# Right operands of w_up without their zero columns, in a transformer layer on one core

## The chip, the core and the metric

The kernel runs on one core of a Trainium2 chip. The core has a matrix engine (TensorE, "PE" in the profile; its weight loads are listed apart as "PEld"), a vector engine (DVE), an activation engine (ACT), a general engine (POOL) and a queue engine (SP) that issues the transfers here. The engines run their own instruction streams in order and wait for each other through semaphores. The metric is the device time of one execution in microseconds (us).

## The reference

One layer of a diffusion backbone is computed for 128 context tokens and 512 latent tokens, 640 in all, 1024 features wide, in float32. After an attention and convolution mixer, the second half of the layer is a feed-forward network with a short convolution over the tokens:

```
def dwconv3(x, w):
    xp = jnp.pad(x, ((0, 0), (1, 1), (0, 0)))
    return w[0] * xp[:, :-2] + w[1] * xp[:, 1:-1] + w[2] * xp[:, 2:]

def conv_ffn(u, p):
    up = dwconv3(u @ p["w_up"], p["conv_ffn"])
    g, val = jnp.split(up, 2, axis=-1)
    return (jax.nn.silu(g) * val) @ p["w_down"]
```

`w_up` is 1024 x 5632, `w_down` 2816 x 1024. The convolution pads each sequence with a zero token at both ends, and context and latent tokens are two sequences. So the rows that are convolved need a zero column ahead of the context, one between context and latent, and one behind the latent.

## The kernel before, in words

*Precision.* Every float32 operand of a large product is split into a high part, rounded to the format that PE multiplies, and a low part, the rest. A product of two such operands is three matmuls (high x high, high x low, low x high) that add up in one PSUM bank. ACT makes the high part (L1017 for weights, L1350 for right operands), DVE the low part (L1021, L1353).

*Layout.* Features lie on the partitions, tokens along the columns. The modulated and normed tokens u, transposed, are written into two tiles `UFa` and `UFb` (features 0 to 511 and 512 to 1023) by `modulated` (L1423). Each row there has `NCOL = 644` columns: a zero, the 128 context tokens, a zero, the 512 latent tokens, two zeros. Six memsets on POOL (L1330 to L1332) write the zeros. Halves of `HALF = 322` columns give four quadrants B11, B12, B21, B22 (first index: features, second: tokens).

*Products.* The 5632 outputs are handled in 22 steps j; each takes 128 columns of the gate half g and 128 of the value half of w_up. The first two (`NPLAIN = 2`) are plain: 16 blocks in all (`plain`, L1466). Steps 2 to 21 use a Strassen scheme with seven blocks instead of eight (`strassen`, L1571): A11, A12, S2, S1, S3, S4, A22 in this order, whose right operands are the quadrants or sums of them (T1 to T4). A block (`block`, L1023) is four k tiles times three matmuls, 12 matmuls of 128 x 128 weights with 322 columns, all issued by line 1030. The same line issues the blocks of an earlier Strassen stage, the projection w_in, with 320 columns (tokens without zeros).

*Banks and sums.* Of step j, two PSUM banks out of a ring of three take the results, and the intermediate results go to the rows of a tile `C` (`crows`, L1459: four rows for g, three for the value, 644 columns each): ACT copies a result to a small tile (`copied`, L1036; tags p1, u2, p5), DVE adds it to the other bank's result and writes half a row of C (`added`, L1040), and the last product of the step, A22, is copied to its half row by ACT in the next step (`last_copy`, L1653). A12 of a step writes over the bank that this copy reads.

*Behind the products.* Three steps later ACT and DVE convolve the rows: ACT multiplies by the middle tap (`tap_mid`, L1507), DVE adds the outer taps (`taps_out`, L1511), then follow silu (L1517), gate times value (`gated`, L1521) and the split of the activations (`act_hi`, `act_lo`). These read `NACT = 642` columns of C, shifted by 0, 1 and 2. From step 4 on, PE also multiplies the activations of step j - 4 by half of w_down (`down`, L1557), 15 matmuls of 512 columns, between S1 and S3. After step 21 the remaining activations and the other half of w_down follow (L1889 on).

*Order.* The instruction order on PE, ACT and DVE is the order in which the code is written (a manual schedule, L263); the copies, sums, splits and taps of a step are therefore interleaved by hand between the calls of `product`. SP's and POOL's orders are set by the framework's scheduler, and so are the waits.

*Memory.* Tiles live in regions that are reused by tag (r0 to r3, r4 to r7b); a region is as long as its longest tile, and the regions lie one behind the other. `C` takes the region of `WR` (r3) when `crows` is called for the first time, in the plain stage.

Of the kernel before, what the change touches and what calls it, by code (L numbers as in the profile page):

```python
# [11 lines left out]
F32 = mybir.dt.float32  # L12
F32R = mybir.dt.float32r
AF = mybir.ActivationFunctionType
ALU = mybir.AluOpType
# [4 lines left out]
NCTX = 128  # L20
NTOK = 640
# [3 lines left out]
NKV = 4  # L25
DFF = 2816
NJ = DFF // 128
NCOL = 644
HALF = NCOL // 2
NACT = NCOL - 2  # L30
NRING = 4
FLAG = 3
DLAG = 4
# [28 lines left out]
def trunk_layer(ctx, tc, x_prompt, x_sample, cache_k, cache_v, c, c_ctx, w_ada, b_ada, g_pre1, g_post1, g_pre2,  # L62
# [3 lines left out]
    V, S, G, PE = nc.vector, nc.scalar, nc.gpsimd, nc.tensor  # L66
# [29 lines left out]
    def region(pool, tag, shape, dtype, name):  # L96
        return pool.tile([128] + shape, dtype, tag=tag, name=name)
# [11 lines left out]
    units += [(w_in, 0, KT, O_GA + j * 128, 128) for j in range(2)] + [(w_att_out, 0, KT, j * 128, 128) for j in range(KT)]  # L109
    rest = [(w_down, 2 * q, 2, 512, 512) for q in (NJ // 2 - 2, NJ // 2 - 1, *range(NJ // 2 - 2))]  # L110
    state = {"next": 0, "raw": [], "cut": [], "limit": 10}
# [77 lines left out]
    hd = dp.tile([NT, 128, D], F32, name="hd")  # L189
    actd = dp.tile([NJ, 128, NACT], F32, name="actd")  # L190

# [73 lines left out]
    with tc.tile_pool(name="pro", bufs=2) as pro, tc.manual_schedule(engines={mybir.EngineType.SP}):  # L265
# [182 lines left out]
        for f in range(KT):  # L448
# [33 lines left out]
            if f == KT - 3:  # L482
                V.tensor_scalar(out=gains[0], in0=gains[0], scalar1=HD ** -0.5, scalar2=None, op0=ALU.mult)
                for i in range(2):
                    for a in range(2):
                        V.tensor_tensor(out=tabs[i][:, :, 0, a * 32:a * 32 + 32], in0=rt[:, :, 0, a * 32:a * 32 + 32],
                                        in1=gains[i][:, :, a * 32:a * 32 + 32].broadcast_to((128, 4, 32)), op=ALU.mult)
                        for hf in range(2):
                            d0, s0 = a * 32 + hf * 16, a * 32 + (1 - hf) * 16
                            V.tensor_tensor(out=tabs[i][:, :, 1, d0:d0 + 16], in0=rt[:, :, 1, d0:d0 + 16],  # L490
                                            in1=gains[i][:, :, s0:s0 + 16].broadcast_to((128, 4, 16)), op=ALU.mult)
            if f == KT - 2:
                cut_upto(9)
                p = ps1()
# [14 lines left out]
    with tc.tile_pool(name="att", bufs=2) as at:  # L509
# [310 lines left out]
        p = ps2()[:, 0:512]  # L820
# [41 lines left out]
        for g in range(NKV):  # L862
            if g and g + 1 < NKV:
                q_begin(g + 1)
            for i in range(0 if g else 1, 9):
# [37 lines left out]
                if blk is not None:  # L903
                    c0, c1 = 256 * blk, min(256 * blk + 256, NTOK)
# [89 lines left out]
    rb = ctx.enter_context(tc.tile_pool(name="rb", bufs=1))  # L994
# [15 lines left out]
    cut, raws, pair, TT = {}, {}, {}, {}  # L1010
# [22 lines left out]
    def temp(tag):  # L1033
        return sm_.tile([128, HALF], F32, tag=tag, name=nm(tag), bufs=1)

# [4 lines left out]
    def added(dst, j, tag, b):  # L1040
        V.tensor_tensor(out=dst, in0=pair[j][b], in1=pair.pop((j, tag)), op=ALU.add)
# [220 lines left out]
    for m, (x, i) in enumerate(PAIRS):  # L1262
# [6 lines left out]
        e, o = 2 * before[1] if m else 0, 2 * before[1] + 1 if m else 0  # L1269
# [7 lines left out]
        elif before[0] == "X":  # L1277
            c0, c1, y0, y1 = ROWS[:4]
# [7 lines left out]
        elif before[0] == "B":  # L1286
            c0, c1, y0, y1, b0, b1 = ROWS[:6]
# [36 lines left out]
    WR = region(ra, "r3", [5, D], F32, "WR")  # L1324
    TX = region(rb, "r4", [5, D], F32, "TX")

    r7 = [rb.tile([128, n], F32, tag=f"r7{x}", name=f"UF{x}") for n, x in ((4 * NCOL, "a"), (3328, "b"))]
    UFS = [x[:, 0:4 * NCOL].rearrange("p (k c) -> p k c", c=NCOL) for x in r7]
    rows3 = r7[1][:, 4 * NCOL:4 * NCOL + 256].rearrange("p (i c) -> p i c", i=2)
    for a, b in ((0, 1), (NCTX + 1, NCTX + 2), (NCOL - 2, NCOL)):  # L1330
        for x in UFS:
            G.memset(x[:, :, a:b], 0.0)  # L1332

    ZB0 = ra.tile([128, 4, 4, HALF], F32R, tag="r0", name="ZB0")
    ZB1 = ra.tile([128, 4, 4, HALF], F32R, tag="r1", name="ZB1")
# [13 lines left out]
    def right_hi(name, src, a=0, b=HALF):  # L1349
        S.activation(TT[name][0][:, :, a:b], QUAD[src][:, :, a:b], AF.Copy)  # L1350

    def right_lo(name, src, a=0, b=HALF):
        V.tensor_tensor(out=TT[name][1][:, :, a:b], in0=QUAD[src][:, :, a:b], in1=TT[name][0][:, :, a:b].bitcast(F32), op=ALU.subtract)  # L1353
# [16 lines left out]
    def ffn_taps(p):  # L1370
# [3 lines left out]

        neg = cffn.rearrange("p (d o) -> p d o", d=3)[:, :, NJ:]
        V.tensor_scalar(out=neg, in0=neg, scalar1=-1.0, scalar2=None, op0=ALU.mult)
# [39 lines left out]
    turned = {}  # L1416
# [5 lines left out]

    def modulated(t, hf):  # L1423
        row = 1 if t == 0 else 0
        c0 = 1 if t == 0 else 2 + t * 128
        for k in range(4):
            f = 4 * hf + k
            dst, src = UFS[hf][:, k, c0:c0 + 128], turned[t, hf][:, k * 128:(k + 1) * 128]
            sc, sh = mod[:, 1, row, f:f + 1], mod[:, 2, row, f:f + 1]
            if k < 3 - hf:  # L1430
                S.activation(dst, src, AF.Identity, scale=sc, bias=sh)
            else:
                V.tensor_scalar(out=dst, in0=src, scalar1=sc, scalar2=sh, op0=ALU.mult, op1=ALU.add)
# [6 lines left out]
    DBANKS = (2, 3, 4, 5, 6)  # L1440
    BANKS = {j: tuple(RING[(2 * (j - NPLAIN) + i) % 3] for i in range(2)) for j in range(NPLAIN, NJ)}
    room = {}
# [4 lines left out]
    def plain_load(j, i):  # L1447
        raws[j, i] = raw_tile()
        up_load(raws[j, i], i * NJ + j)

    def pair_load(j):
        if j < NJ:
            if "raw" not in room:
# [5 lines left out]
    def crows(j):  # L1459
        if "c" not in room:  # L1460
            room["c"] = region(ra, "r3", [7, NCOL], F32, "C")
        return room["c"][:, j % 4, :], room["c"][:, 4 + j % 3, :]

    plain_out = {}
# [5 lines left out]
        block(plain_out[j, tok, i], (j, i), step, f"B{step + 1}{tok + 1}", step == 0, step == 1)  # L1470

    def plain_copy(j, tok, i):
        dst = crows(j)[i][:, tok * HALF:(tok + 1) * HALF]
        S.activation(dst, plain_out[j, tok, i], AF.Copy, scale=(1.0, -1.0)[i])

    def sums(j):

# [93 lines left out]
    def strassen(j):  # L1571

        f, nxt = j - FLAG, j + 1 if j + 1 < NJ else None
        g = NJ - FLAG if nxt is None else None
        cg, cv = crows(j)
        pair[j] = tuple(bank(n)[:, 0:HALF] for n in BANKS[j])
        if j > NPLAIN:
            last_copy(j - 1)
        else:
            plain_copy(1, 1, 1)  # L1580
        if f >= 0:
            tap_mid(f, 0)
        lo_of((j, 1))
        product(j, "A11")

        copied(j, "p1", 0)
        if f >= 0:
            tap_mid(f, 1)
            taps_out(f, 0, (0,))
        product(j, "A12")  # L1590

        hi_of((j, 2), left(j, 2))
        added(cg[:, 0:HALF], j, "p1", 1)
        if f >= 0:
            taps_out(f, 0, (2,))
        lo_of((j, 2))
        product(j, "S2")

        copied(j, "u2", 0)
        if f >= 0:  # L1600
            silu(f)
            taps_out(f, 1)
        product(j, "S1")

        copied(j, "p5", 1)
        hi_of((j, 3), left(j, 3))
        if f >= 0:
            gated(f)
        if nxt:
            adds = sums(nxt)  # L1610
            adds[0]()
        if g:
            cut_upto(len(state["cut"]) + 1)
            tap_mid(g, 0)
            tap_mid(g, 1)
        if j >= DLAG:
            down(j - DLAG)
        product(j, "S3")

        added(cv[:, HALF:], j, "p5", 0)  # L1620
        lo_of((j, 3))
        if nxt:
            pair_load(j + 2)
            hi_of((nxt, 0), left(nxt, 0))
            lo_of((nxt, 0))
            adds[1]()
        q = max((j - DLAG + 1) // 2, 0)
        if j == NPLAIN or (j > DLAG and (j - DLAG) % 2 == 1):
            down_hi(q)
            down_lo(q)  # L1630
            down_load(q + 2 if q else 1)
            if q == 0:
                down_load(2)
        if f >= 0:
            act_hi(f)
        if g:
            act_lo(f)
            taps_out(g, 0)
            silu(g)
        product(j, "S4")  # L1640

        if nxt:
            hi_of((nxt, 1), left(nxt, 1))
        added(cg[:, HALF:], j, "u2", 1)
        if nxt:
            adds[2]()
        if g:
            taps_out(g, 1)
        elif f >= 0:
            act_lo(f)  # L1650
        product(j, "A22")

    def last_copy(j):  # L1653
        S.activation(crows(j)[1][:, 0:HALF], pair[j][0], AF.Copy)


    for row in (1, 0):
# [61 lines left out]
    for t in range(1, NT + 1):  # L1719
        if t >= 2 and t != 4:  # L1720
            normed(t - 2)
        sq_b(t - 1)
        scaled(t - 1, 1)
        for k in (0, 1):
            if t < NT:
                wo_step(t, k)
        if t == NT:
            hi_of((1, 0), raws[1, 0])
            plain(0, 0, 0, 0)
        residual(t - 1)  # L1730
        if t >= 2:
            turn2(t - 2, 0)
            modulated(t - 2, 0)
        for k in (2,):
            if t < NT:
                wo_step(t, k)
        if t == NT:
            plain(0, 0, 0, 1)
        if t >= 2:
            turn2(t - 2, 1)  # L1740
            modulated(t - 2, 1)
        sq_h(t - 1)
        if t == 3:
            right_hi("B11", "11", 0, 258)
            normed(2)
            right_lo("B11", "11", 0, 258)
        if t < NT:
            scaled(t, 0)
        if t == 3:
            right_hi("B21", "21", 0, 258)  # L1750
        if t == 4:
            right_hi("B11", "11", 258, HALF)
            right_lo("B11", "11", 258, HALF)
            right_lo("B21", "21", 0, 258)
            right_hi("B21", "21", 258, HALF)
            right_lo("B21", "21", 258, HALF)
        for k in range(3, KT):
            if t < NT:
                wo_step(t, k)
# [132 lines left out]
    w, x, y = NJ - 3, NJ - 2, NJ - 1  # L1892
# [85 lines left out]
```

## Time and profile before

| | |
|---|---|
| median of 3 runs | 1133.82 us (1132.58 to 1134.37) |
| profiled execution | 1132.64 us |
| span of its profile | 1130.9 us, granted TensorE clock 0.997 |
| w_in in Strassen form | from about 339 to 572 us |
| w_up, plain steps and steps 2, 3 | from about 699 to 744 us |
| w_up, steps 4 to 21 with half of w_down | from about 744 to 1031 us |
| rest of the activations and of w_down | from about 1031 to 1131 us |

The profile is of one execution. Its first part gives the busy time of each engine, the second the span in 40 slices, the fourth the chain of work that ended last, followed back from the end. A row of a group reads: line, engine, operation, tile written <- tiles read, shape, count | busy us, mean ns of one | idle time of the engine just before them, and who ended it. A row of the timeline or the chain reads: start in us from the span's start, length in us, then the same; a bracket behind it gives the idle time before it and its releaser. Matmul rows overlap: the listed length of one runs from its start to its modelled end, while the next one starts well before that.

### The profile page before, as it was taken

The page shows a single profiled execution, that of the slowest core. Times are in us where ns is not written, and L with a number is a line of the kernel's source. Part 1 is how long each engine was busy: PE and PEld are TensorE (multiplying, and loading weights), DVE is VectorE, ACT ScalarE, POOL GpSimd, SP SyncE. Part 2 cuts the span into 40 slices and gives each one's busy share as a digit, 9 for nine tenths or more (in the row PEclk, how much of TensorE's full clock was granted, in tenths as well). Part 3 has the DMA queues.
Part 4 walks back from the last instruction along what each step waited for, and adds up shares of the span by engine and source line. Part 5 has one row for each costly group of instructions (what it writes and reads, how often), then busy time and mean ns, then how long its engine had stood idle before and what let it go on. Part 6 is the DMA issues. An engine that isn't in the chain of part 4 may idle for free.

```text
span 1130.9 us, 19510 instructions
## 1 busy us (share of the span) xinstructions
PE 1112.9 (98%) x7885; PEld 1023.0 (90%) x7885; DVE 794.7 (70%) x1272; ACT 570.0 (50%) x979; POOL 151.5 (13%) x195
## 2 busy tenths in 40 slices
PE   7999999999999999999999999999999999999997
PEld 6787888888999999999999889999999999998786
DVE  4587666664656788889645457888887778888644
ACT  4375666665234454544532256654555455555431
POOL 2056565653000000000000012000000000000001
PEclk9999999999999999999999999999999999999999
DMA  9632433333222223323332644232333233315722
GB/s 338 204 92 79 128 95 113 104 103 113 77 71 78 76 76 96 92 75 89 100 97 77 221 149 157 67 116 88 111 105 107 90 99 106 117 61 185 244 98 93
DMA packets 177304, 129.58 MB, mean 115 GB/s; under 512 B 6274, under 2 KB 159422, under 8 KB 177214
## 3 DMA queue, kind: packets, MB, share of 16 engines
q1 hardware_dynamic: 177102, 128.30, 36.4%
q8 instruction: 62, 1.02, 0.4%
q14 instruction: 28, 0.23, 0.1%
q10 hardware_dynamic: 112, 0.04, 0.0%
HBM read 116.87 MB, written 11.45 MB: 113 GB/s over the span
## 4 chain that ended last, share of the span: by engine, by line
PE 89%; DVE 3%; ACT 1%; issue 0%; POOL 0%; DVEq 0%; POOLq 0%; ACTq 0%
PE b L1030 45%; PE b L159 9%; PE b L157 9%; PE b L158 9%; PE s L789 3%; PE s L765 3%; PE s L589 3%; PE s L157 2%; PE s L158 2%; PE s L159 2%; PE s L209 1%; DVE Y L1514 1%; DVE wlo L693 0%; PE s L560 0%; PE b L1421 0%; DVE mx L727 0%
## 5 line engine op out<-in xcount | busy, mean ns | idle before, releaser
L1030 PE MATMUL b<-ZB,whi 128*128 128x322 f32 x1024 | 228.6, 310 | 0.0
L1030 PEld LDWEIGHTS b<-ZB,whi 128*128 128x128 f32 x1024 | 173.8, 189 | 1.6
L1030 PE MATMUL b<-ZB,wlo 128*128 128x322 f32 x512 | 159.4, 311 | 0.0
L1030 PE MATMUL b<-MT,whi 128*128 128x320 f32 x608 | 134.1, 308 | 0.0
L1030 PEld LDWEIGHTS b<-MT,whi 128*128 128x128 f32 x608 | 101.6, 188 | 0.0
L1030 PEld LDWEIGHTS b<-ZB,wlo 128*128 128x128 f32 x512 | 96.2, 188 | 0.0
L1030 PE MATMUL b<-MT,wlo 128*128 128x320 f32 x304 | 93.8, 308 | 0.0
L752 POOL TENSOR_TENSOR pr<-pr,sm 128x640 f32<-128x640 f32 x64 | 80.6, 1269 | 61.2 <-DVE sm L751 61.2
L1017 ACT ACTIVATE whi<-SUM 128x1024 fp32r<-128x1024 f32 x40 | 42.2, 1055 | 79.6 <-DVE SUM L1484 77.2
L1514 DVE SCALAR_TENSOR_TENSOR Y<-C,cffn,Y 128x642 f32<-128x642 f32 x88 | 77.5, 883 | 0.9
L742 ACT ACTIVATE pr<-s,mx,rq 128x640 f32<-128x640 f32 x64 | 56.7, 886 | 38.5 <-DVE mx L729 36.4
L132 DVE TENSOR_TENSOR wlo<-raw,whi 128x1024 fp32r<-128x1024 f32 (+1 forms) x33 | 36.1, 1094 | 52.5 <-ACT whi L131 52.0
L1030 PE MATMUL b<-UH,whi 128*128 128x320 f32 x228 | 70.5, 309 | 0.0
L1030 PE MATMUL b<-UL,whi 128*128 128x320 f32 x228 | 70.4, 309 | 0.0
L1030 PE MATMUL b<-UH,wlo 128*128 128x320 f32 x228 | 70.2, 308 | 0.0
L1021 DVE TENSOR_TENSOR wlo<-raw,whi 128x1024 fp32r<-128x1024 f32 (+1 forms) x51 | 50.4, 1019 | 25.2 <-ACT whi L1017 24.3
L1017 ACT ACTIVATE whi<-WB 128x1024 fp32r<-128x1024 f32 x38 | 40.1, 1056 | 54.8 <-DVE WB L1125 54.8
L157 PE MATMUL s<-whi,UH 128*128 128x256 f32 (+1 forms) x200 | 65.9, 329 | 0.5 <-ACT UH L376 0.3
L727 DVE TENSOR_REDUCE mx<-s 128x1 f32<-128x640 f32 x64 | 52.5, 820 | 17.5 <-PE s L589 17.2
L158 PE MATMUL s<-wlo,UH 128*128 128x256 f32 (+1 forms) x200 | 61.5, 308 | 2.2 <-DVE wlo L693 2.2
L1038 ACT ACTIVATE p<-b 128x322 f32<-128x322 f32 (+1 forms) x78 | 34.3, 439 | 58.2 <-PE b L1030 58.2
L159 PE MATMUL s<-whi,UL 128*128 128x256 f32 (+1 forms) x200 | 61.8, 309 | 0.2
(319 smaller groups left out, 2922.6 us busy)
## 6 DMA issues: line engine op xcount, KB each, us to landing
raw<-in_w_in_dram SPq DMA_DIRECT2D x48, 512.0 KB, 3.7
RAW<-in_w_up_dram SPq DMA_DIRECT2D x40, 512.0 KB, 3.8
raw<-in_w_ada_dram SPq DMA_DIRECT2D x32, 512.0 KB, 3.9
raw<-in_w_down_dram SPq DMA_DIRECT2D x22, 512.0 KB, 4.0
actd<-Y SPq DMA_DIRECT2D x18, 321.0 KB, 2.6
AFB<-actd SPq DMA_DIRECT2D x18, 321.0 KB, 6.9
XT<-in_w_ada_dram SPq DMA_DIRECT2D x9, 512.0 KB, 8.7
raw<-in_w_conv_out_dram SPq DMA_DIRECT2D x9, 512.0 KB, 4.0
```

The lines of the kernel that those rows point to most:

```text
L132: V.tensor_tensor(out=lo[:, :n], in0=raw, in1=hi[:, :n].bitcast(F32), op=ALU.subtract)
L157: PE.matmul(out, ah, bh, start=start, stop=False)
L158: PE.matmul(out, ah, bl, start=False, stop=False)
L159: PE.matmul(out, al, bh, start=False, stop=stop)
L727: V.tensor_reduce(out=mx, in_=self.sc[h], axis=AX.X, op=ALU.max, negate=True)
L742: S.activation(pr, self.sc[h], AF.Exp, bias=mx, scale=rs, accum_out=sm)
L752: G.tensor_tensor(out=pr, in0=pr, in1=sm.broadcast_to((128, NTOK)), op=ALU.mult)
L1017: S.activation(to[0], raw, AF.Copy)
L1021: V.tensor_tensor(out=lo, in0=raw, in1=hi.bitcast(F32), op=ALU.subtract)
L1030: PE.matmul(out, p[:, ws], q[:, k, :], start=start and k == 0 and n == 0, stop=stop and k == 3 and n == 2, skip_group_check=True)
L1038: S.activation(t, pair[j][b], AF.Copy)
L1514: V.scalar_tensor_tensor(out=y, in0=crows(j)[i][:, d:d + NACT], scalar=cffn[:, 44 * d + o:44 * d + o + 1], in1=y, op0=ALU.mult, op1=ALU.add)
```

## The change

The right operands lose their zero columns: `UFa` and `UFb` have 640 columns, all tokens, `HALF` is 320, and each block's matmuls have 320 columns. The zeros are written only in the seven rows of `C`, once, by three memsets on POOL when C is first used. Since the first token half now holds the 128 context tokens and 192 latent tokens without the zero between them, a result for that half goes into its row in two pieces, 128 columns at column 1 and 192 at column 130 (`PARTS`); the second half is one piece of 320 at column 322. This touches the plain copies (`plain_copy`), the step's sums (`added_to` in place of `added`, for w_up only) and `last_copy`. The early splits of a part of B11 and B21 are 256 columns in place of 258. Order of the instructions, banks, transfers and counts of matmuls are as before.

```diff
+HALF = NTOK // 2
+
 NCOL = 644
-HALF = NCOL // 2
 NACT = NCOL - 2
+PARTS = (((0, 128, 1), (128, 320, 130)), ((0, 320, 322),))
...
-    r7 = [rb.tile([128, n], F32, tag=f"r7{x}", name=f"UF{x}") for n, x in ((4 * NCOL, "a"), (3328, "b"))]
-    UFS = [x[:, 0:4 * NCOL].rearrange("p (k c) -> p k c", c=NCOL) for x in r7]
...
-    for a, b in ((0, 1), (NCTX + 1, NCTX + 2), (NCOL - 2, NCOL)):
-        for x in UFS:
-            G.memset(x[:, :, a:b], 0.0)
+    r7 = [rb.tile([128, n], F32, tag=f"r7{x}", name=f"UF{x}") for n, x in ((4 * NTOK, "a"), (3328, "b"))]
+    UFS = [x[:, 0:4 * NTOK].rearrange("p (k c) -> p k c", c=NTOK) for x in r7]
...
     def crows(j):
         if "c" not in room:
             room["c"] = region(ra, "r3", [7, NCOL], F32, "C")
+            for a, b in ((0, 1), (NCTX + 1, NCTX + 2), (NCOL - 2, NCOL)):
+                G.memset(room["c"][:, :, a:b], 0.0)
...
     def plain_copy(j, tok, i):
-        dst = crows(j)[i][:, tok * HALF:(tok + 1) * HALF]
-        S.activation(dst, plain_out[j, tok, i], AF.Copy, scale=(1.0, -1.0)[i])
+        for a, b, c in PARTS[tok]:
+            S.activation(crows(j)[i][:, c:c + b - a], plain_out[j, tok, i][:, a:b], AF.Copy, scale=(1.0, -1.0)[i])
...
-        added(cg[:, 0:HALF], j, "p1", 1)
+        added_to(cg, 0, j, "p1", 1)
...
-        added(cv[:, HALF:], j, "p5", 0)
+        added_to(cv, 1, j, "p5", 0)
...
-        added(cg[:, HALF:], j, "u2", 1)
+        added_to(cg, 1, j, "u2", 1)
...
+    def added_to(row, tok, j, tag, b):
+        t = pair.pop((j, tag))
+        for a, e, c in PARTS[tok]:
+            V.tensor_tensor(out=row[:, c:c + e - a], in0=pair[j][b][:, a:e], in1=t[:, a:e], op=ALU.add)
+
     def last_copy(j):
-        S.activation(crows(j)[1][:, 0:HALF], pair[j][0], AF.Copy)
+        for a, b, c in PARTS[0]:
+            S.activation(crows(j)[1][:, c:c + b - a], pair[j][0][:, a:b], AF.Copy)
```

More of the change, by code (lines that the diff above doesn't have):

```diff
@@ L1325, in trunk_layer @@
     TX = region(rb, "r4", [5, D], F32, "TX")
-    r7 = [rb.tile([128, n], F32, tag=f"r7{x}", name=f"UF{x}") for n, x in ((4 * NCOL, "a"), (3328, "b"))]
-    UFS = [x[:, 0:4 * NCOL].rearrange("p (k c) -> p k c", c=NCOL) for x in r7]
-    rows3 = r7[1][:, 4 * NCOL:4 * NCOL + 256].rearrange("p (i c) -> p i c", i=2)
-    for a, b in ((0, 1), (NCTX + 1, NCTX + 2), (NCOL - 2, NCOL)):
-        for x in UFS:
-            G.memset(x[:, :, a:b], 0.0)
+    r7 = [rb.tile([128, n], F32, tag=f"r7{x}", name=f"UF{x}") for n, x in ((4 * NTOK, "a"), (3328, "b"))]
+    UFS = [x[:, 0:4 * NTOK].rearrange("p (k c) -> p k c", c=NTOK) for x in r7]
+    rows3 = r7[1][:, 4 * NTOK:4 * NTOK + 256].rearrange("p (i c) -> p i c", i=2)
     ZB0 = ra.tile([128, 4, 4, HALF], F32R, tag="r0", name="ZB0")
@@ L1424, in modulated @@
         row = 1 if t == 0 else 0
-        c0 = 1 if t == 0 else 2 + t * 128
         for k in range(4):
             f = 4 * hf + k
-            dst, src = UFS[hf][:, k, c0:c0 + 128], turned[t, hf][:, k * 128:(k + 1) * 128]
+            dst, src = UFS[hf][:, k, t * 128:(t + 1) * 128], turned[t, hf][:, k * 128:(k + 1) * 128]
             sc, sh = mod[:, 1, row, f:f + 1], mod[:, 2, row, f:f + 1]
@@ L1743, in trunk_layer @@
         if t == 3:
-            right_hi("B11", "11", 0, 258)
+            right_hi("B11", "11", 0, 256)
             normed(2)
-            right_lo("B11", "11", 0, 258)
+            right_lo("B11", "11", 0, 256)
         if t < NT:
@@ L1749, in trunk_layer @@
         if t == 3:
-            right_hi("B21", "21", 0, 258)
+            right_hi("B21", "21", 0, 256)
         if t == 4:
[L1752 to L1756, printed above, removed]
+            right_hi("B11", "11", 256, HALF)
+            right_lo("B11", "11", 256, HALF)
+            right_lo("B21", "21", 0, 256)
+            right_hi("B21", "21", 256, HALF)
+            right_lo("B21", "21", 256, HALF)
         for k in range(3, KT):
```

## The prediction

> **What bounds the kernel now.** I read the page's shares and slices first, then the waits of TensorE (PE), the chain that ended last, and the groups of PE by shape. From the page:
>
> ```profile
> span 1130.9 us, 19510 instructions
> PE 1112.9 (98%) x7885; PEld 1023.0 (90%) x7885; DVE 794.7 (70%) x1272; ACT 570.0 (50%) x979; POOL 151.5 (13%) x195
> ...
> PEclk9999999999999999999999999999999999999999
> ...
> PE 89%; DVE 3%; ACT 1%; issue 0%; POOL 0%; DVEq 0%; POOLq 0%; ACTq 0%
> ```
>
> PE is busy nearly always, at full granted clock, and carries 89% of the chain. A busy matmul row overlaps its neighbours (a mean of 310 ns below, yet a new one about every 148 ns), so busy time says nothing of the pace; the chain does, since it follows the starts. Its long pieces (start, length, count):
>
> ```profile
> 339.52 232.60 PE b L1030 x1586
> ...
> 699.34 51.87 PE b L1030 x348
> 754.70 12.48 PE b L1030 x84
> ...
> 1010.30 12.48 PE b L1030 x84
> 1026.27 1.81 PE b L1030 x12
> 1028.11 0.49 DVE C L1041
> ```
>
> The first piece is the earlier projection (w_in), whose products run through the same line and the same form of tile, 320 columns each: 232.60 / 1586 = 146.66 ns. The 17 pieces of 84 are the steps of w_up at 322 columns: 12.48 / 84 = 148.57 ns. This pair decides most of the forecast: same engine, weights of the same size, same split into three products, same clock, two columns apart, 1.91 ns apart. The 348 are the plain steps and the first three Strassen steps, 149.05 ns each, with small waits inside. The last two rows show PE handing the chain to DVE inside the final step. The groups that change, from the groups by form:
>
> ```profile
> L1030 PE MATMUL b<-ZB,whi 128*128 128x322 f32 x1024 | 228.6, 310 | 0.0
> L1030 PE MATMUL b<-ZB,wlo 128*128 128x322 f32 x512 | 159.4, 311 | 0.0
> ...
> L1030 PE MATMUL b<-ZT,whi 128*128 128x322 f32 x160 | 36.3, 313 | 0.0
> L1030 PE MATMUL b<-ZT,wlo 128*128 128x322 f32 x80 | 24.8, 311 | 0.0
> L1030 PE MATMUL b<-ZB,ZB 128*128 128x322 f32 x84 | 13.4, 312 | 0.0
> L1030 PE MATMUL b<-ZB 128*128 128x322 f32 x12 | 2.0, 313 | 0.0
> ```
>
> Together 1872, as the code has it: 16 plain blocks and 20 x 7 Strassen blocks of 12. None of these groups idles before a matmul.
>
> **The change part by part.**
>
> *Two columns less in 1872 products.* Nothing of the count, the order or the weights changes. If these products take the pace of the 320-column ones, 1872 x 1.91 = 3.57 us. The other way to price it is by the slope between widths. Between these two rows lie eleven starts of products of 512 columns:
>
> ```profile
> 799.70 0.39 PE L157 MATMUL b<-WD,ACTa 128*128 128x512 f32 x1
> ...
> 802.24 0.39 PE L159 MATMUL b<-WD,ACTb 128*128 128x512 f32 x1
> ```
>
> 2.54 / 11 = 231 ns, so (231 - 146.66) / 192 = 0.44 ns a column, 0.88 ns for two, 1.64 us for 1872. By that slope a product of 322 columns would take 147.5 ns; it takes 148.57, so the odd width costs about 1 ns more than its columns. A row of 322 floats is 1288 bytes and each k starts at another offset; 320 is what the other piece has. I take 3.57, because the 1586 products are the nearest rows: same line, same tiling, same neighbours. Both ends stay for the range; the upper end is 1872 x (149.05 - 146.66) = 4.5, were the small waits of the first steps to go too. Of the 1872, the last 24 (S4 and A22 of the final step) run after the chain has passed to DVE: less 0.05.
>
> [...]
>
> *One piece more per step on ACT and on DVE.* Each step's copy of the previous step's last product (L1654) and its first sum (L1041, the p1 one) become two instructions, 128 and 192 wide; so do the four plain copies for the first token half: 24 more on ACT, 20 more on DVE. Groups that give a fixed cost, all reading PSUM:
>
> ```profile
> L1041 DVE TENSOR_TENSOR C<-b,p 128x322 f32<-128x322 f32 x40 | 19.7, 492 | 52.3 <-PE b L1030 51.8 <-ACT whi L1017 0.4
> L1388 DVE TENSOR_TENSOR TX<-b,WR 128x512 f32<-128x512 f32 x10 | 6.8, 684 | 4.3 <-ACT TX L1399 4.3
> L1433 DVE TENSOR_SCALAR UFb<-b,mod 128x128 f32<-128x128 f32 x10 | 3.6, 407 | 2.2 <-ACT UFb L1431 2.2
> L1654 ACT ACTIVATE C<-b 128x322 f32<-128x322 f32 x20 | 8.4, 421 | 0.0
> L1431 ACT ACTIVATE UFb<-b,mod 128x128 f32<-128x128 f32 x10 | 4.1, 459 | 1.1 <-PE b L1421 1.1
> L1399 ACT ACTIVATE TX<-b 128x512 f32<-128x512 f32 x5 | 3.0, 598 | 4.8 <-PE b L159 4.8
> ```
>
> DVE: (684 - 492) / 190 = 1.01 ns an element, so 492 - 325 = 167 ns fixed; the 128-wide row, another form with scale and shift from memory, has 407, 278 fixed. ACT: (598 - 421) / 190 = 0.93 ns an element, 121 ns fixed, and 340 from the 128-wide form. I take 0.16 us a piece, near the rows of the same form, with 0.3 as the upper end; the lower end is about 0.05, as neighbours on a queue overlap. In a steady step (DVE, then ACT):
>
> ```profile
> 772.58 0.49 DVE L1041 TENSOR_TENSOR C<-b,p 128x322 f32<-128x322 f32 x1 [2.62 <-PE b L1030]
> 780.14 0.48 DVE L1041 TENSOR_TENSOR C<-b,p 128x322 f32<-128x322 f32 x1
> 776.50 0.42 ACT L1654 ACTIVATE C<-b 128x322 f32<-128x322 f32 x1
> 777.88 0.44 ACT L1038 ACTIVATE p<-b 128x322 f32<-128x322 f32 x1 [0.24 <-PE b L1030]
> 781.43 0.44 ACT L1038 ACTIVATE u<-b 128x322 f32<-128x322 f32 x1 [1.44 <-PE b L1030]
> ```
>
> The copy ends at 776.92, and A12, which writes over its bank, starts just before A11's result is copied at 777.88: about 0.8 us of cover for 0.16. Behind it on ACT stand a tap and the p copy, which has 0.24 us of idle time; were it late, S2 needs it only a product (12 x 148.57 = 1.8 us) later. On DVE the sum that is split is the one at 780.14. It reads the bank that S1 overwrites; S1 starts when S2's result is copied, at about 781.4, so 0.7 us of cover. What stands behind it (a tap, then the low half for S3) is read a product later still, and DVE idles 2.62 us once a step, so nothing adds up from step to step. Zero in steps 5 to 21; without the cover 0.16 us each.
>
> The cover is thin in one place, step 3, which has no w_down work to give DVE time. DVE, then weight loads:
>
> ```profile
> 735.08 0.49 DVE L1041 TENSOR_TENSOR C<-b,p 128x322 f32<-128x322 f32 x1 [0.24 <-PE b L1030]
> 741.61 1.81 DVE L1021 TENSOR_TENSOR wlo<-RAW,whi 128x512 fp32r<-128x512 f32 x2
> 742.35 0.19 PEld L1030 LDWEIGHTS b<-ZT,wlo 128*128 128x128 f32 x1 [0.24 <-DVE wlo L1021]
> 745.11 0.42 ACT L1654 ACTIVATE C<-b 128x322 f32<-128x322 f32 x1
> ```
>
> From the p1 sum at 735.08 to the low half at 741.61 DVE runs without a gap, and PE already waits 0.24 us for it. The sum is the instruction that is split, so the wait grows by 0.16, and by 0.09 more because the 48 products between get 1.91 ns shorter each: 0.25 us lost. The copy of step 4 at 745.11 is late behind it and may hold A12: 0 to 0.2, I take 0.1.
>
> *The zeros.* Six memsets on POOL go and three on the tile C come:
>
> ```profile
> L1332 POOL MEMSET UFa<- 128x4 f32 x2 | 0.1, 106 | 332.4 <-DVE MLa L1044 332.4
> ```
>
> A tenth of a us each; POOL does nothing between 699 and 1026 us, no copy into C touches the zero columns, and their first reader is the tap of step 3, some 30 us later. Zero; uncovered, 0.3 once. SP's order of transfers is untouched: zero.
>
> *Smaller tiles.* Right operands, their sums and splits are 0.6% shorter: some ns each on engines off the chain, zero. Several regions become 32 or 64 bytes shorter, so later tiles move; one of them (r6b) also feeds 228 products of w_in. At 1.91 ns each, the one penalty of offsets seen here, that is at most 0.4 us of loss; I take zero and keep it for the range.
>
> Sum: 3.57 - 0.05 - 0.25 - 0.10 = 3.2 us. The profiled execution took 1132.64 us (span 1130.9), so 1129.4 for one like it. The median of the runs, 1133.82, lies 1.2 us above that execution; against it the forecast is 1130.6.
>
> **The rivals.**
> *Only the columns count.* The 1 ns above the slope belongs to this stage (its w_down products and transfers in between) and not to the width. Then 1.64 - 0.4 = 1.2 us, 1132.6. For it: the slope from 320 to 512 columns. Against it: the pieces of 84 have no other product among them.
> *The weight load sets the pace.* PEld is busy 90% and every product loads new weights; then nothing is gained, 1133.8 to 1134.2. Against it: weights are equal at 320 and 512 columns, and the pace is 147 and 231 ns.
> *Slower: the second pieces reach PE.* Place: DVE's sum and ACT's copy at the head of each step. If both pieces came through, 20 x 0.32 = 6.4 against 3.5: +2.9, 1136.7. It decides from 0.18 us a step upwards. For it: step 3 as it is. The Trainium skill, "Perfetto Trace Analysis", section "Optimizing Scalar/DVE Operations", charges each such instruction its own overhead and advises grouping, which speaks against splitting; the fixed costs above agree. Against it: from step 5 on each piece has over 0.4 us of cover.
>
> **How the numbers follow.** A change of 0.2%, 2.3 us, is about what can be told from none. Forecast 0.72, its own range 1129.3 (4.5 us) to 1131.5; columns only 0.16; weight load 0.05; slower 0.07. The first is faster by over 0.2%, the next two are within it. The range takes in the columns-only case and the runs' own spread (1132.58 to 1134.37): 1128.5 to 1133.2.
>
> **What would show it.** Right: the pieces of 84 in the chain come to 12.32 us, the span of steps 5 to 21 shrinks by 0.16 us each, and the wait before A22 of step 3 grows to about 0.5. Wrong: pieces of 12.40 (columns only) or 12.48; new rows in which PE waits for C's copies or sums in the steady steps; or the earlier 1586 products above 146.7 ns.

## The result, and the profile after

The changed kernel takes 1128.64 us (median of 6 runs, 1128.48 to 1130.06) against 1133.21 us of the kernel before beside it (6 runs, 1132.47 to 1134.48). The ratio is 0.9964, with a 95% interval of 0.9953 to 0.9974: faster by 0.36%, some 4.1 us by the ratio. The forecast had 3.2 us and 1130.6, with a range down to 1128.5.

The page of the changed kernel's profiled execution (1128.51 us) begins:

```profile
span 1126.7 us, 19577 instructions
...
PE 1107.7 (98%) x7885; PEld 1017.2 (90%) x7885; DVE 795.8 (71%) x1292; ACT 571.3 (51%) x1003; POOL 151.4 (13%) x192
```

As many matmuls as before, 20 more instructions on DVE and 24 on ACT, three fewer on POOL. PE still carries the span, which is 4.2 us shorter. The long pieces of its chain (start, length, count; line 1032 is what was 1030):

```profile
339.78 232.93 PE b L1032 x1596
...
698.45 51.46 PE b L1032 x348
753.40 12.31 PE b L1032 x84
...
1006.25 12.31 PE b L1032 x84
1022.05 1.77 PE b L1032 x12
1023.85 0.49 DVE C L1656
```

The same view of the kernel before, now over the whole of w_in (the prediction's row stops at 572 us, ten products before its end):

```profile
339.52 234.07 PE b L1030 x1596
```

So the 4.2 us can be laid out stage by stage, by the starts of the pieces in the two executions:

| stretch | before | after | gained |
|---|---|---|---|
| to the first block of w_in | 339.52 | 339.78 | -0.26 |
| 1596 products of w_in (code unchanged) | 234.07 | 232.93 | 1.14 |
| from there to the 348 of w_up | 125.75 | 125.74 | 0.0 |
| 348 products of w_up, then the first w_down | 55.36 | 54.95 | 0.41 |
| from the first piece of 84 to the last 12 | 271.57 | 268.65 | 2.92 |
| rest of the span | 104.6 | 104.6 | 0.0 |

The pieces of 84 take 12.31 us, within 0.01 of the forecast, and 17 of them give the 2.9 us. The surprise is the second row: 1.14 us in a stage that the change does not touch.

The thin place of the forecast, step 3 and the head of step 4, in the changed kernel (DVE, weight loads, ACT):

```profile
733.75 0.56 DVE L1656 TENSOR_TENSOR C<-b,p 128x128 f32<-128x128 f32 x2
...
741.08 0.19 PEld L1032 LDWEIGHTS b<-ZT,wlo 128*128 128x128 f32 x1 [0.24 <-DVE wlo L1023]
...
743.84 0.48 ACT L1660 ACTIVATE C<-b 128x128 f32<-128x128 f32 x2
```

Two pieces take 0.56 us on DVE where one took 0.49, and 0.48 us on ACT where one took 0.42: 0.07 and 0.06 us a piece, under half of the 0.16 in the sum. The wait before this load is still 0.24 us. But the matmuls just ahead of it are spread out as well: from the starts in the two traces, the matmuls around A22 of step 3 lose 0.38 us against an even pace, where it was 0.24, and the first of A12 in step 4 loses 0.07. So 0.2 us were lost there, not 0.35.

### The profile page after: what moved, and what is told of

Same layout as the page of the kernel before. It is cut to its first block, busy times and chain, and to the rows that moved or that the text cites. A ratio compares the mean times of both kernels' runs of the same rounds, so it can differ in the third digit from the quotient of the medians.

```text
span 1126.7 us, 19577 instructions
## 1 busy us (share of the span) xinstructions
PE 1107.7 (98%) x7885; PEld 1017.2 (90%) x7885; DVE 795.8 (71%) x1292; ACT 571.3 (51%) x1003; POOL 151.4 (13%) x192
## 4 chain that ended last, share of the span: by engine, by line
PE 88%; DVE 3%; ACT 1%; POOL 0%; issue 0%; DVEq 0%; POOLq 0%; ACTq 0%
PE b L1032 44%; PE b L161 9%; PE b L159 9%; PE b L160 9%; PE s L791 3%; PE s L767 3%; PE s L591 3%; PE s L159 2%; PE s L161 2%; PE s L160 2%; PE s L211 1%; DVE Y L1514 1%; DVE wlo L695 0%; PE s L562 0%; PE b L1420 0%
## 5 line engine op out<-in xcount | busy, mean ns | idle before, releaser
L1032 PE MATMUL b<-ZB,whi 128*128 128x320 f32 x1024 | 225.9, 308 | 0.0
L1032 PE MATMUL b<-ZB,wlo 128*128 128x320 f32 x512 | 157.8, 308 | 0.0
L1040 ACT ACTIVATE p<-b 128x320 f32<-128x320 f32 x78 | 34.2, 438 | 53.9 <-PE b L1032 52.1
```

Of the source, the lines that this page charges most:

```text
L1032: PE.matmul(out, p[:, ws], q[:, k, :], start=start and k == 0 and n == 0, stop=stop and k == 3 and n == 2, skip_group_check=True)
L1040: S.activation(t, pair[j][b], AF.Copy)
```

## The experiments

Single executions differ by up to 2.7 us before the first block of w_in (it starts between 339.30 and 342.03 us in the profiles below), in work that is the same in all of them. So the stages are compared by the pieces of the chain, which repeat to some hundredths.

**Every tile at its old place.** The changed kernel's tiles are a little shorter, and so later tiles start elsewhere. Here they are padded to the old lengths:

```diff
-        return sm_.tile([128, HALF], F32, tag=tag, name=nm(tag), bufs=1)
+        return sm_.tile([128, 322], F32, tag=tag, name=nm(tag), bufs=1)[:, 0:HALF]
...
-    ZB0 = ra.tile([128, 4, 4, HALF], F32R, tag="r0", name="ZB0")
+    ZB0 = ra.tile([128, 16 * 322], F32R, tag="r0", name="ZB0")[:, 0:16 * HALF].rearrange("p (a k c) -> p a k c", a=4, k=4)
...
```

> The changed kernel with the regions r0, r1, r2, r5a, r6a and the three small tiles padded to their old lengths, so that every tile lies where it lay before the change; nothing else differs. Theory (places set part of the pace): the products of w_in, whose code the change does not touch, go back from 232.93 us for 1596 in the chain to about 234.07, the pieces of 84 of w_up stay at 12.31 us, and the whole takes about 1.1 us more than the changed kernel, about 1129.7. Rival 1 (the w_in difference is chance between two executions): w_in stays at 232.9, time about 1128.6. Rival 2 (places, not the width, made the w_up products faster): the pieces of 84 go back to 12.4 or more.

Its chain:

```profile
339.85 234.07 PE b L1032 x1596
...
699.57 51.44 PE b L1032 x348
754.51 12.31 PE b L1032 x84
770.32 12.30 PE b L1032 x84
```

w_in is back at 234.07, to the hundredth, and w_up keeps its gain. So the 1.14 us come from where tiles lie, and the gain in w_up does not. The time was 1129.0 us (1128.92 to 1129.52), ratio 0.9965 (0.9952 to 0.9978); by the times alone it can't be told from the changed kernel, by this stage it can (the two profiled executions, 1129.52 and 1128.51 us, differ by 1.0).

**T4 alone moved by 32 bytes.** Of the operands of w_in, T4 in region r6b is the only one whose start changes its place within 64 bytes. Here it starts 32 bytes further on, with all else where the changed kernel has it:

```diff
-        z = rb.tile([128, 2, 4, HT], F32R, tag=tag, name=f"M{name}")
+        z = rb.tile([128, 2, 4, HT], F32R, tag=tag, name=f"M{name}") if name != "T4" else \
+            rb.tile([128, 8 + 8 * HT], F32R, tag=tag, name="MT4")[:, 8:].rearrange("p (a k c) -> p a k c", a=2, k=4)
```

> The changed kernel with the fourth sum operand of w_in (T4 in region r6b) alone moved by 32 bytes, back to a start at a multiple of 64 bytes as it had before the change; nothing else moves. Theory (this 32 byte move is what made w_in faster): w_in back to about 234.1 us for 1596, everything else as in the changed kernel. Rival (another of the moved tiles): 232.9.

```profile
342.03 234.67 PE b L1032 x1596
...
702.44 51.47 PE b L1032 x348
757.40 12.31 PE b L1032 x84
```

234.67: this move alone takes back the gain and 0.6 us more. The rival falls, but the expected 234.1 is missed as well: with T4 at a multiple of 64 bytes w_in takes 234.07 us when all tiles lie at their old places and 234.67 here, so something else about the places counts too. It isn't T4's own block that changes, though. From the starts in the traces, the medians from one start to the next (ns) in the 12 matmuls of block A12 of w_in, whose operand, weights and bank lie elsewhere, and the mean over the seven blocks A11, A12, S2, S1, S3, S4, A22:

```
before        A12: 147 148 146 146 148 146 146 148 146 146 148 146   blocks: 147.3 146.8 146.7 146.5 146.2 146.7 146.4
changed       A12: 140 147 146 140 148 146 140 148 146 140 147 146   blocks: 145.6 144.5 146.4 147.0 146.8 145.0 146.8
T4 moved      A12: 145 147 152 153 148 143 145 147 147 145 148 152   blocks: 147.9 147.7 147.7 147.0 147.0 146.3 147.1
```

In the changed kernel every third start of A12 comes 6 or 7 ns early, and so do two of A11 and three of S4; with T4 moved that is gone.

**320 columns out of rows of 322.** Is it the width of the instruction that matters, or the offset at which each row starts?

```diff
-                PE.matmul(out, p[:, ws], q[:, k, :], start=start and k == 0 and n == 0, stop=stop and k == 3 and n == 2,
+                PE.matmul(out, p[:, ws], q[:, k, 0:W], start=start and k == 0 and n == 0, stop=stop and k == 3 and n == 2,
...
```

with `W = 320`, the sums and copies of the same width, and zeros in the columns of C that no copy fills.

> The kernel before with its tiles as they were, rows of 322 columns, but each product of w_up reads only the first 320 of them; sums and copies stay in one piece. It leaves out the last two columns of each half, so two latent tokens count as zero in the convolution. Theory of the prediction (the odd width costs about 1 ns beside its columns, through the starting offsets of the rows): the offsets are still there, so the pieces of 84 take about 12.40 us. Rival (only the number of columns in an instruction matters, and 320 has the good pace wherever its rows start): 12.31. Rival (columns cost nothing here): 12.48.

```profile
339.45 234.07 PE b L1031 x1596
...
754.17 12.34 PE b L1031 x84
```

12.34, not 12.40. Of the 0.17 us between 12.48 and 12.31, the number of columns gives 0.14 and the offsets of the rows 0.03. The forecast's mechanism, that the offsets make the odd width dear, falls; its price stands. Why 322 columns cost more than two columns above 320 stays open.

**Fewer columns still.** The same kernel with W = 318, 316, 312 and 304. Each product now takes the width of its result (`q[:, k, 0:out.shape[1]]`), so that those of w_in keep their 320 columns.

> As e2_320_of_322 (rows of 322, all tiles at their old places, one piece), but each product of w_up reads 318 columns; it leaves out the last four columns of each half. At 322 columns the pieces of 84 took 12.48 us, at 320 from the same rows 12.34. If a column costs 0.44 ns throughout and 322 carried 1 ns extra for not being a round number of columns, 318 carries it as well and gains nothing: about 12.35. If the cost is a straight line near 320 with the slope from 322 to 320 (0.07 us a column): 12.20. If it follows 0.44 ns a column without extra below 320: 12.27.

> As e7_318_of_322, with 316 columns read by each product of w_up; the last six columns of each half are left out. 318 and 320 columns took the same (pieces of 84: 12.32 to 12.34 us), 322 took 12.48, so the pace goes in steps and not along a line. Steps of 4 columns at 0.44 ns a column: 12.19. Steps of 8 or 16: 12.33. A floor below 320 columns set by something else than the width: 12.33 here and in the two runs below as well.

> As above with 312 columns; ten columns of each half are left out. Steps of 4 or 8 columns: 12.04 us for the pieces of 84. Steps of 16: 12.33. A floor: 12.33.

> As above with 304 columns; eighteen columns of each half are left out. Steps of any size up to 16 columns: about 11.74 us for the pieces of 84 (84 x 16 x 0.44 ns less than 12.33). A floor: 12.33.

The chains, two neighbouring pieces of each kernel, 318 first:

```profile
756.22 12.34 PE b L1031 x84
772.04 12.32 PE b L1031 x84
```

```profile
753.87 12.27 PE b L1031 x84
769.60 12.28 PE b L1031 x84
```

```profile
755.90 12.14 PE b L1031 x84
771.54 12.17 PE b L1031 x84
```

```profile
753.33 11.81 PE b L1031 x84
768.64 12.00 PE b L1031 x84
```

322, 320, 318, 316, 312, 304 columns: 12.48, 12.34, 12.33, 12.27, 12.15, and for 304 pieces that alternate between 11.81 and about 12.0. The alternation is a wait and not the pace: in the eight longer pieces, and only there, PE stands still once for the low half that DVE makes for S2, eight times with 1.5 us in all. One of the eight:

```profile
777.29 0.19 PEld L1031 LDWEIGHTS b<-ZB,wlo 128*128 128x128 f32 x1 [0.18 <-DVE wlo L1022]
```

So 11.81 is the pace of 304 columns. No floor, and none of the expected steps of 4, 8 or 16: the width does cost, but two columns are worth 0.14 us at 322, 0.01 at 320 and 0.06 at 318. From 322 to 304 it is 0.67 us for 18 columns, 0.44 ns a column and matmul, as much as between 320 and 512. The slope is right over a long way and says little about two columns.

**Five pieces.** Do the added pieces have cover?

```diff
-PARTS = (((0, 128, 1), (128, 320, 130)), ((0, 320, 322),))
+PARTS = (((0, 64, 1), (64, 128, 65), (128, 192, 130), (192, 256, 194), (256, 320, 258)), ((0, 320, 322),))
```

> The changed kernel with the first token half written in five pieces of 64 in place of two (128 and 192): three more instructions on ACT and three more on DVE per step, about 0.16 us each by the prediction's price, 0.5 us per engine and step. Theory (the pieces have cover from step 5 on, none in steps 3 and 4): the pieces of 84 stay within 0.02 us of 12.31, the waits of step 3 and 4 grow by about 0.5 us each, and the time rises by about 1 us against the changed kernel. Rival (pieces reach PE): 0.3 to 1 us more in every step, the time rises by 6 to 20 us.

Its chain, then its weight loads that waited, a sum of step 3 on DVE and the copy of step 4 on ACT:

```profile
754.81 12.31 PE b L1032 x84
...
1023.46 1.77 PE b L1032 x12
```

```profile
741.77 0.30 PEld L1032 LDWEIGHTS b<-ZT,whi 128*128 128x128 f32 x2 [0.33 <-ACT ACTa L1529]
742.30 0.19 PEld L1032 LDWEIGHTS b<-ZT,wlo 128*128 128x128 f32 x1 [0.24 <-DVE wlo L1023]
745.78 0.30 PEld L1032 LDWEIGHTS b<-ZB,whi 128*128 128x128 f32 x2 [0.25 <-ACT C L1660]
```

```profile
741.17 0.48 DVE L1656 TENSOR_TENSOR C<-b,p 128x320 f32<-128x320 f32 x1
...
745.07 0.66 ACT L1660 ACTIVATE C<-b 128x64 f32<-128x64 f32 x5
```

The same sum and the load behind it in the changed kernel:

```profile
739.94 0.48 DVE L1656 TENSOR_TENSOR C<-b,p 128x320 f32<-128x320 f32 x1
...
740.54 0.30 PEld L1032 LDWEIGHTS b<-ZT,whi 128*128 128x128 f32 x2
```

From 754.81 to 1023.46 are 268.65 us, exactly what the changed kernel needs: in the steady steps three more pieces on each engine cost nothing. In steps 3 and 4 PE waits. The second and third row name the two instructions that the prediction named there, the low half on DVE and the copy on ACT. The first row names an instruction of ACT that had ended at 741.38. But A22 adds to the bank that the DVE sum of 741.17 reads, and this load starts 0.12 us after that sum ends, as it does in the changed kernel; so this wait fits DVE's queue, which the added pieces delay, better than ACT's. The added 0.35 us (55.30 against 54.95 from the 348 on) is less than the 1 us expected, since a piece costs 0.06 us and not 0.16 (five take 0.66).

**One piece.** The other direction:

```diff
-PARTS = (((0, 128, 1), (128, 320, 130)), ((0, 320, 322),))
+PARTS = (((0, 320, 1),), ((0, 320, 322),))
...
-            for a, b in ((0, 1), (NCTX + 1, NCTX + 2), (NCOL - 2, NCOL)):
+            for a, b in ((0, 1), (HALF + 1, HALF + 2), (NCOL - 2, NCOL)):
```

> The changed kernel with the first token half written in one piece of 320 at column 1 again, so that copies and sums are as many as before the change. It leaves out the zero column between context and latent tokens, so the convolution runs across that border. Theory: the pieces of 84 stay 12.31 us and w_in 232.9; the second piece cost something in steps 3 and 4 alone, so the 348 products of the plain and first Strassen steps take 0.15 to 0.3 us less than the changed kernel's 51.46, and the first product after step 3 no longer finds PE held up by the copy. Rival (the pieces cost something in every step that the shorter products hide): the pieces of 84 fall below 12.28.

```profile
700.46 51.35 PE b L1032 x348
755.29 12.31 PE b L1032 x84
```

12.31 again, and 51.35 in place of 51.46: the second piece costs 0.11 us once, less than the 0.15 to 0.3 expected, and nothing per step. By the starts, the matmuls around A22 of step 3 still lose 0.31 us here, and those of A12 in step 4 only 0.01. So of the 0.2 us lost in the changed kernel about 0.1 is the second piece; the rest comes with the shorter products alone, for which the forecast had 0.09.

**The low parts 64 bytes further.** The 7 ns above suggested that the distance between the high and the low part of an operand decides, since in the changed kernel's w_in that distance had changed by 64 bytes. First all right operands of w_up, then only the six in r0 to r2, so that no other tile moves (`PAD = 16` floats between the high and the low parts):

```diff
+    def shifted(z, n):
+        m = 4 * HALF
+        at = [i * m for i in range(n)] + [n * m + PAD + i * m for i in range(n)]
+        return [z[:, a:a + m].rearrange("p (k c) -> p k c", k=4) for a in at]
...
-        TT[i] = (z[:, a], z[:, a + 1])
+        TT[i] = (z[a // 2], z[2 + a // 2])
...
```

> The changed kernel with the low parts of all right operands of w_up moved 64 bytes further behind the high parts. In the changed kernel's w_in stage the low parts of the untouched operands lie 64 bytes (in 128) off the high parts, and there the blocks A11, A12 and S4 show every third start 140 ns after the one before, where it was 146 to 148 with the old places. Theory (the distance of low and high part decides this): w_up's blocks show the 140 ns too, the pieces of 84 take about 12.15 us, and the time falls by about 3 us against the changed kernel, to about 1125.5. Rival (the pattern comes from something else, such as the weights' places): 12.31, no change in time.

```profile
339.67 234.21 PE b L1033 x1596
...
754.44 12.26 PE b L1033 x84
770.19 12.28 PE b L1033 x84
```

> As e5_low_64, but the two operands in r5a and r6a keep their form, so that no other tile moves against the changed kernel; only the low parts of the six operands in r0 to r2 lie 64 bytes later. In e5_low_64 the pieces of 84 fell to 12.26 to 12.32 us while w_in rose from 232.93 to 234.21, though its operands and weights lay where they were in the changed kernel. Theory (w_in's pace hangs on the tiles that e5_low_64 moved as well, and w_up's on the low parts): w_in 232.9, pieces of 84 about 12.27, time about 0.7 us under the changed kernel. Rival (the two are coupled in another way): w_in at 234 again.

```profile
339.85 232.95 PE b L1033 x1596
...
753.25 12.28 PE b L1033 x84
769.04 12.29 PE b L1033 x84
```

The first kernel misses what was expected of it (12.15 us), the second meets its own expectation. In both A11, A12 and S4 of w_up do get faster (146.3 or less, 144.5 and 145.2 ns, where the changed kernel has 147.0, 147.0 and 147.2), but the other blocks do not follow, and the pieces gain 0.03 us, not 0.16. And the first kernel loses w_in, though the low parts there keep their distance to the high parts. The second expectation holds that its operands lay still, but they did not: with longer tiles in r5a and r6a, T2 and T3 of w_in start 64 bytes later and T4 96, which brings T4 back to a multiple of 64 bytes and fits the T4 experiment. So the distance of high and low part is not the rule for all blocks. The second kernel keeps both gains: 1127.97 us (1127.91 to 1128.24), ratio to before 0.9949 (0.9933 to 0.9966). By its pieces it is 17 x 0.03 = 0.5 us ahead of the changed kernel; the intervals of the two overlap.

## Why the prediction came out as it did

- *Direction and mechanism* were right. PE sets the time, the products of 320 columns run at the pace that the 1586 of w_in showed, and the pieces came out at 12.31 us where 12.32 was forecast. That the pieces agree to 0.01 us is in part luck: with other places of the operands the same 320 columns took 12.26 to 12.32 us. The median lies just inside the lower end of the range, and this is luck too: the range had been drawn for w_up and the runs' own spread, not for a gain in w_in.
- *The reason given for the price* was wrong. The row offsets, named as the cause of the extra 1 ns, hold 0.03 of 0.17 us; the rest comes with the count of columns in the instruction (320 of 322), by a mechanism that no run shows. The choice of the nearest rows over the slope was sound all the same: with the slope, 1.64 us would have come out for these products; they gave 3.3 (2.92 and 0.41, small losses in steps 3 and 4 included).
- *Smaller tiles* was the term that was mis-sized: it was put at zero, with at most 0.4 us of loss kept for the range. It gave 1.14 us of gain. The place was named (r6b, fed to w_in), but the bound was taken from one penalty seen and put on one side only, and only for T4's own products. The T4 run shows that a start 32 bytes off changes blocks that do not read it. This term, less 0.26 us by which the changed kernel's execution came later to w_in, makes most of the difference between 3.2 and 4.2.
- *The pieces*: 0.06 to 0.07 us each in place of 0.16, no cost in steps 5 to 21 (five pieces: 268.65 us both times), about 0.2 us lost in steps 3 and 4 in place of 0.35. The wait before A22's low half did not grow to 0.5; it stayed 0.24, and the loss showed in the starts beside it.
- *The rivals*: "only the columns count" as a slope is refuted by 12.31 and by the widths; "the weight load sets the pace" by 304 columns at 11.81 us with the same weights; "the pieces reach PE" by five pieces. What the Trainium skill's page "Perfetto Trace Analysis" (section "Optimizing Scalar/DVE Operations") says of an overhead for each instruction agrees with the 0.06 to 0.07 us measured in that there is one. There the Trainium skill advises grouping for an engine that is saturated, a condition that the prediction left out: here DVE is busy 71% and ACT 51% of the span, and from step 5 on the pieces cost no time.

## What to carry to other kernels

Price a narrower matmul by products of exactly that width elsewhere in the same trace, not by a slope between far widths: two columns were worth anything from 0.01 to 0.14 us in 84 products. Where PE sets the pace, splitting a copy or sum on an engine with cover cost nothing here (five pieces, 268.65 us as with two), and the place to look is the one step whose cover is thin. And when a change shortens tiles, expect other stages to change pace by some tenths of a per cent because their operands have moved: compare stage by stage before a gain is put down to the edit.

## What the runs showed of the hardware that had not been expected

- The pace of a stage of matmuls depends on where its operands start, to 32 bytes: 1596 products took 234.07, 232.93 and 234.67 us with T4 at three places (the first of them with other tiles moved as well), and the figure repeats to 0.04 us from execution to execution in kernels with the same places. Which property of a place is good isn't settled: the distance of high and low part explains some blocks and not others.
- A shift of 32 bytes in one operand changes the spacing of matmuls that do not read it (A12: four of twelve starts 140 ns after the one before, with T4 moved none under 143). How it reaches them was not tried further.
- Around 320 columns the pace of products is not a straight line in the width: 84 of them took 12.48, 12.34, 12.33 and 12.27 us with 322, 320, 318 and 316 columns read from the same rows, while the mean from 322 to 304 is 0.44 ns a column.
